# The end of a mixture-of-experts layer: products of the last two pairs in another order, the last norm on other engines, the branch behind the output

## The chip, the cores and the metric

The kernel runs on one core of a Trainium2 chip. The metric is device time in microseconds (us), lower is better. A core has five engines with a queue each: TensorE (PE, with its weight loads as PEld), VectorE (DVE), ScalarE (ACT), GpSimd (POOL) and SyncE (SP), which here issues the DMAs. Matrix products write to PSUM, eight banks of 128 x 512 float32; all else lies in SBUF.

## What is computed

One layer over 256 rows of 1024 numbers: a mixer (gated linear attention and retention), a layer norm, a mixture of 32 experts of which each row takes four, and a last layer norm. The end of it is what the change touches:

```python
h = layer_norm(DEEPNORM_ALPHA * h + mix, ln1_g[l], ln1_b[l])
ffn = moe_ffn(h, router_w[l], router_b[l], moe_w1[l], moe_b1[l], moe_w2[l], moe_b2[l])
h = layer_norm(DEEPNORM_ALPHA * h + ffn.astype(h.dtype), ln2_g[l], ln2_b[l])

# one expert e with the rows xb that chose it
hh = xb @ w1[e] + b1[e]                                  # 1024 -> 2048
x_glu = jnp.minimum(hh[:, :D_FF], SWIGLU_LIMIT)
x_lin = jnp.clip(hh[:, D_FF:], -SWIGLU_LIMIT, SWIGLU_LIMIT)
act = x_glu * jax.nn.sigmoid(SWIGLU_ALPHA * x_glu) * (x_lin + 1.0)
return act @ w2[e] + b2[e]                               # 1024 -> 1024, then times the gate, summed over experts
```

The weights of the experts are 32 x (8 MB + 4 MB) of float32, some 403 MB of the 424 MB that the kernel moves.

## The kernel before

**Pairs.** Two experts make a pair; there are 16, and each expert has 64 seats (CAP), so that a pair fills 128 partitions. For a pair p the work is: `begin` (`gather`, L746) picks the rows by products with a 0/1 matrix; `hidden` is the first product, 8 steps k of 4 blocks of 512 columns, each block a `pair_product` (L767), which is two float32 matmuls that stand side by side in 64 output rows each; `activate` (L813 to L817, DVE and ACT) is the clamped SwiGLU; `turn` (L824, L825) transposes the result on PE and copies it out on ACT; `outputs` is the second product, 4 steps g of 2 x 2 `pair_product`s into two banks, copied to `y` by ACT (L842); `gated` (L850 to L856) makes the transposed gates, and `scatter` (L879, L883) multiplies them with `y` and adds the result to the sum `acc`, 256 rows in two tiles t. The scatter of pair p - 1 (`finish`) runs inside the first product of pair p, after its step k = 1.

**What sets the order.** `in_order` chains all PE work in the order of the program's text. The other engines are ordered by a scheduler that works from dependencies, and `tc.issue_after` forces the order of two instructions where it is used.

**The stream.** SP issues the weights as DMAs of 1 MB (L960 for w1, L962 for w2; one of each expert makes a step), eight in flight, into 20 slots of 1 MB that come round as a ring; a slot is free again when the products that read it are done.

**The last pair before.** Its w2 comes in 24 smaller pieces (L987): first all of the columns 0:512 in 8 pieces of 512 KB, then 512:768 and 768:1024 in 16 pieces of 256 KB (rows of 1 KB), so that a column block of the result is finished before the next one has arrived. Each block is evicted (L1000, L1013), scattered and put through the statistics of the last norm (L886) in turn.

**The branch and the last norm.** An expert with more than 64 rows needs further rounds. All engines load a count (`values_load`, L1017) and branch (`tc.If(count > CAP)`, L1022) over the code for these rounds; with the inputs here none is needed. Behind the branch stands the last norm (L1060 to L1078): aggregate, logarithm and exponential, a Newton step (`newton`, L173 to L177), then four tiles of 128 x 512, three of them on DVE (two instructions each, L1077 and L1078), one on ACT and POOL (L1072 to L1074), and an output DMA for each (L1079). L1119 is the end of the program, where the engines meet.

Of the kernel before, what the change touches and what calls it, by code (L numbers as in the profile page):

```python
# [33 lines left out]
WARM = (10, 8, 6)  # L34
NS = 20
# [8 lines left out]
def tile_layer(ctx: ExitStack, tc: tile.TileContext, x, positions, rows_d, bc_d, gate_d, w_in, wglr_d,  # L44
# [736 lines left out]
    def hidden(xg, sel2, load, name, mid=None, early=None, bias_last=False):  # L781
# [20 lines left out]
        if mid:  # L802
            mid()
        aT = mp.tile([P, KC, P], F32, name="aT" + name, tag="aT")
        for turn in turns_:
            turn(aT)
        return aT, bsel, sigs[-1]

    def activate(hf, ps, name):
# [3 lines left out]
        V.tensor_scalar(glu, pglu, 7.0, None, op0=ALU.min)  # L813
# [3 lines left out]
        V.scalar_tensor_tensor(glu, plin, 1.0, glu, op0=ALU.add, op1=ALU.mult)  # L817
# [3 lines left out]
        def turn(aT):  # L821
            pa = bank("y", f"pa{name}{hf}").rearrange("p (k s) -> p k s", k=4)
# [6 lines left out]
    def outputs(aT, bsel, load, name):  # L829

        y = mp.tile([P, D], F32, name="y" + name, tag="y")
        py = [bank("y", f"py{name}{n}") for n in range(2)]
        for n in range(2):
            set_bias(py[n], bsel, 4 + n)
        for g in range(4):
            ws = [load("w2", i, g) for i in range(2)]
            for k in range(2):
                for n in range(2):
                    pair_product(py[n], aT, 2 * g + k, [w.rearrange("p (k n) -> p k n", k=2)[:, k, n * 512:(n + 1) * 512] for w in ws],
                                 g == 3 and k == 1)  # L840
        for n in range(2):
# [29 lines left out]
    st2 = const.tile([P, NT, 4, 6], F32, name="st2")  # L871
# [3 lines left out]
    def scatter(y, gT, at, n, name, stats=False, tag="m", first=False):  # L875

        for t in range(NT):
# [6 lines left out]
            if stats:  # L884
                for c in range(at, at + n, 256):
                    V.bn_stats(st2[:, t, c // 256, :], acc[:, t, c:c + 256])  # L886
# [67 lines left out]
    for p in range(NP):  # L954
        nm = f"_{p}"

        def load(what, i, g):
            w = slot(next_slot(), f"{what}{nm}{i}_{g}")
# [6 lines left out]

        if p:
# [3 lines left out]
        if p == NP - 2:  # L970
            kept = next_slot()
            gb2 = row_slot(kept, G2, "gb2")
        aT, bsel, last_sig = hidden(xgs[p], sel[:, 2 * p:2 * p + 2], load, nm, mid=(lambda: begin(p + 1)) if p + 1 < NP else None,
                                    early=lambda: middle(p), bias_last=(p == 0))
        if p + 1 < NP:
            ys[p] = outputs(aT, bsel, load, nm)
            continue

        loads = []

        def load_pair(ws, w, k0, m, c_):

            n, w_k = ws[0].shape[-1], ws[0].shape[1]
            for kq in range(0, w_k, m):
                for i in range(2):
                    with tc.issue_after(loads[-1].ins) if loads else ExitStack():
                        loads.append(nc.sync.dma_start(  # L987
                            ws[i][:, kq:kq + m, :],
                            w[0, 2 * p + i][(k0 + kq) * P:(k0 + kq + m) * P, c_:c_ + n].rearrange("(p k) n -> p k n", p=P)))

        preload(EXPLN, last_sig)
        y = mp.tile([P, D], F32, name="y" + nm, tag="y")
        py = bank("y", "py_last0")
        set_bias(py, bsel, 4)
        for kh in range(2):
            ws = [slot(next_slot(), f"w2{nm}{i}_0{kh}").rearrange("p (k n) -> p k n", k=4) for i in range(2)]
            load_pair(ws, moe_w2, 4 * kh, 2, 0)
            for k in range(4):
                pair_product(py, aT, 4 * kh + k, [w[:, k, :] for w in ws], kh == 1 and k == 3)
        A.activation(y[:, 0:512], py, AF.Copy)  # L1000
        for q in range(2):
            at = 512 + 256 * q
            py = bank("y" if q == 0 else "h", f"py_last{q + 1}")[:, 0:256]
            ws = [slot(next_slot(), f"w2{nm}{i}_1{q}").rearrange("p (k n) -> p k n", k=8) for i in range(2)]
            load_pair(ws, moe_w2, 0, 2, at)
            set_bias(py, bsel, 5, 256 * q)
            for k in range(8):
                if q == 0 and k == 4:
                    scatter(y, gTs[p], 0, 512, nm, stats=True)
                if q == 1 and k == 6:  # L1010
                    scatter(y, gTs[p], 512, 256, nm, stats=True)
                pair_product(py, aT, k, [w[:, k, :] for w in ws], k == 7)
            A.activation(y[:, at:at + 256], py, AF.Copy)  # L1013
        scatter(y, gTs[p], 768, 256, nm, stats=True)
# [5 lines left out]
    free = [s_ for s_ in ring if s_ != kept]  # L1020
    chain[0] = None
    with tc.If(count > CAP):  # L1022
        for r in range(1, S // CAP):
            V.tensor_scalar(pos, pos, -float(CAP), None, op0=ALU.add)
            with tc.For_i(0, NP, 1) as p:
# [16 lines left out]
                aT, bsel, _ = hidden(xg, sel[:, 0:2], load, nm)  # L1042
                y = outputs(aT, bsel, load, nm)
# [3 lines left out]
                for tl in (pos, gate, sel):  # L1047
# [4 lines left out]
                    V.tensor_copy(tl, tmp)  # L1052
        for t in range(NT):
            for c in range(4):
                V.bn_stats(st2[:, t, c, :], acc[:, t, c * 256:(c + 1) * 256])
        preload(EXPLN, A.activation(nmr2, st2[:, 0, 0, 0:1], AF.Copy))


    for t in range(NT):
# [63 lines left out]
```

## Time and profile before

| | us |
|---|---|
| time, median of 3 runs (1083.78 to 1084.68) | 1084.24 |
| the profiled execution: its time | 1084.73 |
| the profiled execution: its span in the trace | 1082.9 |
| PE busy (share of the span) | 1009.8 (93%) |
| DVE busy | 273.1 (25%) |
| ACT busy | 168.9 (16%) |
| POOL busy | 36.1 (3%) |
| moved by DMA, 424.17 MB, mean GB/s | 392 |

All times of the trace are us from the start of the span. "Busy" is the time in which an engine executes; the granted clock is what the chip allows TensorE, 1.00 for 2.4 GHz and 0.50 for 1.2 GHz. A row of a timeline gives start, duration, engine, line, operation, what is written and read, the shapes and how many instructions it groups; in brackets stands the idle time before it and what ended that. A matmul of float32 leaves two records, and a `pair_product` four.

### The profile page before, as it was taken

What the parts mean: (1) busy time and instruction counts of PE and PEld (TensorE: products, weight loads), DVE (VectorE), ACT (ScalarE), POOL (GpSimd) and SP (SyncE); (2) the same over time, 40 slices, a digit from 0 to 9 for tenths busy, and PEclk for the clock granted to TensorE, in tenths of its full rate; (3) what the DMA queues carried; (4) which work ended last, traced back from release to release, by engine and by line L of the source; (5) the groups of instructions that cost most, each with busy time, mean ns of one, the idle gap of its engine ahead of it and who ended that gap; (6) DMA issues with size and microseconds to landing.
All of it is one profiled execution on the core that took longest, in us unless ns stands there. A gap on an engine that the chain in (4) does not pass through costs nothing. (4 is left out here: it accounts for less than half of the span.)

```text
span 1082.9 us, 11976 instructions
## 1 busy us (share of the span) xinstructions
PE 1009.8 (93%) x4870; PEld 457.6 (42%) x4870; DVE 273.1 (25%) x574; ACT 168.9 (16%) x350; POOL 36.1 (3%) x90
## 2 busy tenths in 40 slices
PE   8999999999999999999989899998989898999974
PEld 6989844343434342434333243433333332434322
DVE  5667832121212123212120111212121101212114
ACT  3755521010101010101010010101010010101010
POOL 2001100000000000000000000000000000000001
PEclk9999999999999998999999999999999999989997
DMA  9866789999999999999999999999999999999993
GB/s 340 312 238 223 303 339 419 420 420 420 419 419 419 420 419 419 419 419 419 420 420 419 421 420 419 419 419 419 420 420 420 419 419 420 420 419 419 419 371 118
DMA packets 70706, 424.17 MB, mean 392 GB/s; under 512 B 7300, under 2 KB 11887, under 8 KB 22511
## 3 DMA queue, kind: packets, MB, share of 16 engines
q1 hardware_dynamic: 70496, 422.78, 95.9%
q8 instruction: 40, 0.66, 0.3%
q10 hardware_dynamic: 146, 0.53, 0.1%
q14 instruction: 24, 0.20, 0.1%
HBM read 421.71 MB, written 1.05 MB: 390 GB/s over the span
## 5 line engine op out<-in xcount | busy, mean ns | idle before, releaser
L767 PE MATMUL ph<-w,xg 128*64 128x512 f32 x2048 | 469.3, 601 | 31.1 <-DMA w<-in_moe_w_dram 31.1
L767 PEld LDWEIGHTS ph<-w,xg 128*64 128x64 f32 x2048 | 152.0, 138 | 338.9 <-issue 270.2
L767 PE MATMUL py<-w,aT 128*64 128x512 f32 x960 | 218.2, 613 | 0.0
L883 DVE TENSOR_TENSOR acc<-acc,po 128x512 f32<-128x512 f32 (+1 forms) x62 | 41.6, 671 | 391.5 <-PE po L879 391.4
L767 PEld LDWEIGHTS py<-w,aT 128*64 128x64 f32 x960 | 69.7, 141 | 138.9 <-issue 138.4
L813 DVE TENSOR_SCALAR glu<-ph 128x512 f32<-128x512 f32 x32 | 22.0, 687 | 333.5 <-PE ph L767 314.5
L814 ACT ACTIVATE ph<-glu 128x512 f32<-128x512 f32 x32 | 19.3, 602 | 540.2 <-DVE glu L813 540.2
L746 PEld LDWEIGHTS px<-hot,res 128*128 128x128 f32 x512 | 58.4, 192 | 12.5 <-DVE glu L816 10.6
L746 PE MATMUL px<-hot,res 128*128 128x128 f32 x512 | 61.6, 278 | 0.7 <-DVE hot L752 0.7
L879 PE MATMUL po<-y,gT 128*128 128x512 f32 (+1 forms) x132 | 59.8, 594 | 0.5 <-ACT y L1013 0.5
L842 ACT ACTIVATE y<-py 128x512 f32<-128x512 f32 x30 | 17.9, 598 | 217.5 <-PE py L767 217.5
L879 PEld LDWEIGHTS po<-y,gT 128*128 128x128 f32 x132 | 23.6, 189 | 36.0 <-issue 34.9
L759 ACT ACTIVATE xg<-px,cols 128x128 f32<-128x128 f32 x64 | 24.1, 458 | 44.6 <-PE px L746 44.6
L773 PE MATMUL py<-bt,bsel 64*128 64x512 f32 x30 | 14.8, 498 | 16.9 <-ACT aT L825 16.9
L778 POOL CAST bsel<-sel 128x128 fp32r<-128x128 f32 x16 | 4.7, 291 | 634.1 <-PE py L773 624.2
L815 DVE TENSOR_SCALAR ph<-ph 128x512 f32<-128x512 f32 x32 | 22.2, 694 | 2.2 <-PE ph L767 1.2
L761 DVE TENSOR_SCALAR xg<-px,cols 128x128 f32<-128x128 f32 x64 | 21.8, 403 | 3.4 <-PE px L746 3.4
L824 PE MATMUL pa<-ident,glu 128*128 128x128 f32 x128 | 18.6, 286 | 3.8 <-DVE glu L817 3.8
L817 DVE SCALAR_TENSOR_TENSOR glu<-ph,glu 128x512 f32<-128x512 f32 x32 | 22.0, 686 | 0.7
L816 DVE TENSOR_TENSOR glu<-glu,ph 128x512 f32<-128x512 f32 x32 | 21.6, 678 | 0.9 <-ACT ph L814 0.7
L850 POOL TENSOR_TENSOR hog<-hot,gate 128x128 f32<-128x128 f32 x32 | 12.6, 415 | 218.5 <-PE pg L854 205.1
L824 PEld LDWEIGHTS pa<-ident,glu 128*128 128x128 f32 x128 | 16.7, 207 | 5.3 <-DVE glu L817 5.3
(290 smaller groups left out, 658.9 us busy)
## 6 DMA issues: line engine op xcount, KB each, us to landing
w<-in_moe_w_dram SPq DMA_DIRECT2D x376, 1024.0 KB, 19.9
w_out<-in_w_out_dram SPq DMA_DIRECT2D x4, 1024.0 KB, 8.0
w<-in_moe_w_dram SPq DMA_DIRECT2D x8, 512.0 KB, 15.7
w<-in_moe_w_dram SPq DMA_DIRECT2D x16, 256.0 KB, 6.2
w_gqk<-in_w_in_dram SPq DMA_DIRECT2D x2, 1024.0 KB, 9.5
w_rqk<-in_w_in_dram SPq DMA_DIRECT2D x2, 1024.0 KB
w_gv<-in_w_in_dram SPq DMA_DIRECT2D x2, 1024.0 KB, 10.6
w_rv<-in_w_in_dram SPq DMA_DIRECT2D x2, 1024.0 KB, 14.4
```

Of the source, the lines that this page charges most:

```text
L746: in_order(lambda: T.matmul(px[c // 4][:, c % 4, :], res[:, t, c * P:(c + 1) * P], hot[:, t, :], start=(t == 0 and c % 4 == 0), stop=(t == ...
L759: lasts["xa"] = A.activation(xg[:, c, :], px[c // 4][:, c % 4, :], AF.Identity, bias=bs, scale=gs)
L761: lasts["xv"] = V.tensor_scalar(xg[:, c, :], px[c // 4][:, c % 4, :], gs, bs, op0=ALU.mult, op1=ALU.add)
L767: in_order(lambda: T.matmul(ps[i * CAP:(i + 1) * CAP, :], lhs[:, k, i * CAP:(i + 1) * CAP], ws[i], start=first, stop=last, skip_group_chec ...
L813: V.tensor_scalar(glu, pglu, 7.0, None, op0=ALU.min)
L814: sig = A.activation(pglu, glu, AF.Sigmoid, scale=1.702)
L815: V.tensor_scalar(plin, plin, 7.0, -7.0, op0=ALU.min, op1=ALU.max)
L816: V.tensor_mul(glu, glu, pglu)
L817: V.scalar_tensor_tensor(glu, plin, 1.0, glu, op0=ALU.add, op1=ALU.mult)
L824: in_order(lambda: T.transpose(pa[:, k, :], units[:, k // 2, k % 2, :], ident))
L879: in_order(lambda: T.matmul(po[:, 0:n], gT[:, t, :], y[:, at:at + n], start=True, stop=True))
L883: V.tensor_add(acc[:, t, at:at + n], acc[:, t, at:at + n], po[:, 0:n])
```

## The change

The diff below stands for these edits:

- The order of the last two pairs is now: first product of pair 14, first product of pair 15, second product of pair 14, second product of pair 15. What waits meanwhile is held in `waiting`; the transposes of pair 14 go into pair 15's first product after k = 1 (through banks of tag "m"), those of pair 15 into the middle of pair 14's second product (`between`), to a slot of the ring (`ay_last`).
- The w2 of pair 15 comes in four whole DMAs of 1 MB (half the rows), then the other half of the rows in 6 pieces of 512 KB and 4 of 256 KB that have 512 columns each (rows of 2 KB).
- The columns 512:1024 of the sum are gathered in two PSUM banks, `fused`: identity times `acc`, plus the scattered results of pair 14, plus those of pair 15. The statistics read these banks.
- The last norm leaves POOL out. For the tile t = 1 PE multiplies the centred rows by a diagonal matrix `dg` of the reciprocal deviations on top of the bias row (in `pz`), and ACT copies the result out; for t = 0 DVE does both steps. Ten transposes with no use for the result stand ahead of it on PE (`WARM2`).
- The outputs go out before the count is loaded and the branch is taken; ACT first copies `fused` to `acc` for the rounds behind the branch, and a second copy of the norm stands there.
- In all pairs the DVE instructions of the second half of `activate` are forced behind those of the first.

```diff
-        aT = mp.tile([P, KC, P], F32, name="aT" + name, tag="aT")
-        for turn in turns_:
-            turn(aT)
-        return aT, bsel, sigs[-1]
+        return turns_, bsel, sigs[-1]
...
-        V.tensor_scalar(glu, pglu, 7.0, None, op0=ALU.min)
+        with tc.issue_after(last_act[0].ins) if hf else ExitStack():
+            V.tensor_scalar(glu, pglu, 7.0, None, op0=ALU.min)
...
+        def early():
+            if p < NP - 1:
+                middle(p)
+            else:
+                waiting[0:0] = turned(waiting.pop(0), waiting[-1], "m")
...
+        if p < NP - 2:
+            ys[p] = outputs(*turned(turns_, nm), biased(bsel, nm), load, nm)
+        elif p == NP - 2:
+            waiting = [turns_, biased(bsel, nm), load, nm]
...
+    fused = [bank("m", f"fused{t}") for t in range(NT)]
+    def between():
+        both.extend(turned(turns_, nm, "h", slot(next_slot(), "ay_last")))
+        for t in range(NT):
+            in_order(lambda: T.matmul(fused[t], ident, acc[:, t, 512:D], start=True, stop=False, skip_group_check=True))
+    ys[L - 1] = outputs(*waiting, between=between)
...
+    for g in range(2):
+        ws = [load("w2", i, g).rearrange("p (k n) -> p k n", k=2) for i in range(2)]
+        for k in range(2):
+            for n in range(2):
+                pair_product(py[n], aT, 2 * g + k, [w[:, k, cs[n]] for w in ws])
+        if g == 0:
+            scatter(y_old, gTs[L - 1], 0, 512, "_old", tag="y")
+            for t in range(NT):
+                in_order(lambda: T.matmul(fused[t], gTs[L - 1][:, t, :], y_old[:, 512:D], start=False, stop=False, skip_group_check=True))
...
+        for k in range(4):
+            if n and k == 2:
+                scatter(y, gTs[L], 0, 512, "_last", stats=True, tag="y")
+            pair_product(py[n], aT, 4 + k, [w[:, k, :] for w in ws], k == 3)
+        A.activation(y[:, cs[n]], py[n], AF.Copy)
+    for t in range(NT):
+        in_order(lambda: T.matmul(fused[t], gTs[L][:, t, :], y[:, 512:D], start=False, stop=True, skip_group_check=True))
+        V.bn_stats(st2[:, t, 1, :], fused[t])
...
+    for _ in range(WARM2):
+        in_order(lambda: T.transpose(warm2[:, 0:P], ident, ident))
...
+        centre(1, 0)
+        after(lambda: newton(r, small("ln2_w" + name, 2, "_w"), ve))
+        A.activation(dg, ident, AF.Copy, scale=r[:, 1:2])
+        centre(1, 1)
+        for n in range(2):
+            in_order(lambda: T.matmul(pz[n], dg, u[:, 1, cs[n]], start=False, stop=True, skip_group_check=True))
+            lasts["out"] = A.activation(ob[:, 1, cs[n]], pz[n], AF.Copy)
+            nc.sync.dma_start(out[0, P:2 * P, cs[n]], ob[:, 1, cs[n]])
+        for n in range(2):
+            centre(0, n)
+            after(lambda: V.scalar_tensor_tensor(ob[:, 0, cs[n]], u[:, 0, cs[n]], r[:, 0:1], gb2[:, 1, cs[n]], op0=ALU.mult, op1=ALU.add))
+            nc.sync.dma_start(out[0, 0:P, cs[n]], ob[:, 0, cs[n]])
...
+    norm_out(lambda t, n: fused[t] if n else acc[:, t, cs[0]], "")
+    with tc.issue_after(lasts["out"].ins):
+        for t in range(NT):
+            A.activation(acc[:, t, 512:D], fused[t], AF.Copy)
     count = nc.values_load(routed[0][0:1, 0:1], min_val=0, max_val=S)
```

Where PE stands between the pairs 14 and 15 before: `px` is the gather of pair 15, `pa` the transposes and `py` the second product of pair 14 (`w_140` and `w_141` are weights of its two experts, `aT` its activated rows).

```order
L746 MATMUL px_5099<-hot_5096,res 128x128 x4
L824 MATMUL pa_5127<-ident,glu_5084 128x128 x4
L824 MATMUL pa_5133<-ident,glu_5090 128x128 x4
L773 MATMUL py_5140<-bt,bsel_4954 128x512
L773 MATMUL py_5141<-bt,bsel_4954 128x512
L767 MATMUL py_5140<-w_140_0_5144,aT_5126 64x512
L767 MATMUL py_5140<-w_141_0_5146,aT_5126 64x512
```

The same place on PE with the change: `pg` are the gates and `ph` the first product of pair 15 (`w_150`, `w_151`).

```order
L747 MATMUL px_5099<-hot_5096,res 128x128 x4
L774 MATMUL py_5126<-bt,bsel_4954 128x512
L774 MATMUL py_5127<-bt,bsel_4954 128x512
L869 MATMUL pg_5133<-ident,hog_5130 128x128 x2
L774 MATMUL ph_5140<-bt,bsel_5138 128x512
L774 MATMUL ph_5141<-bt,bsel_5138 128x512
L774 MATMUL ph_5142<-bt,bsel_5138 128x512
L774 MATMUL ph_5143<-bt,bsel_5138 128x512
L768 MATMUL ph_5140<-w_150_0_5148,xg_5097 64x512
L768 MATMUL ph_5140<-w_151_0_5150,xg_5097 64x512
```

Behind the gather PE now goes on with the first product of pair 15, and the transposes of pair 14 have left this place.

The end of PE's work before, from the last two matmuls of the last pair's last block on:

```order
L767 MATMUL py_last_5417<-w_150_11_5418,aT_5332 64x256
L767 MATMUL py_last_5417<-w_151_11_5419,aT_5332 64x256
L879 MATMUL po_5454<-y_5346,gT_5200 128x256
L879 MATMUL po_5458<-y_5346,gT_5200 128x256
L1017 TENSOR_LOAD mosti
L1022 COMPARE_AND_BRANCH
```

The same with the change:

```order
L768 MATMUL py_last_5339<-w_150_c_5389,ay_last 64x512
L768 MATMUL py_last_5339<-w_151_c_5390,ay_last 64x512
L1049 MATMUL fused_5271<-ay_last,gT_5136 128x512
L1049 MATMUL fused_5272<-ay_last,gT_5136 128x512
L1057 MATMUL pz_5418<-gb_4952,ones 128x512
L1057 MATMUL pz_5419<-gb_4952,ones 128x512
L1060 MATMUL warm_5422<-ident 128x128 x10
L1087 MATMUL pz_5418<-u,dg 128x512
L1087 MATMUL pz_5419<-u,dg 128x512
L1102 TENSOR_LOAD mosti
L1107 COMPARE_AND_BRANCH
```

The part of the norm that is now PE's, its bias rows and the ten transposes stand between the last scatter and the branch.

The end of SP's queue before; the branch L1022 stands ahead of all these rows, right behind the last weights, and the L1038 and L1025 rows are the code that it jumps over:

```order
L1038 DMA w_r_3_6224<-in_moe_w_dram 128x2048
L1025 REGISTER_ALU
L1025 COMPARE_AND_BRANCH
L1025 UNCONDITIONAL_BRANCH
L1022 UNCONDITIONAL_BRANCH x2
L1079 DMA out_dram<-acc 128x512 x4
L1119 UNCONDITIONAL_BRANCH
```

The end of SP's queue with the change, from the last weights on:

```order
L1042 DMA w_150_c_5389<-in_moe_w_dram 128x512
L1042 DMA w_151_c_5390<-in_moe_w_dram 128x512
L1093 DMA out_dram<-out 128x512
L1089 DMA out_dram<-out 128x512 x2
L1093 DMA out_dram<-out 128x512
L1107 COMPARE_AND_BRANCH
L1110 COMPARE_AND_BRANCH
L1110 UNCONDITIONAL_BRANCH x2
```

The outputs now follow the weights, and the jump is SP's last step instead of one between the two.

## Rows read from the trace of the kernel before

**Rows 1.** Windows: stretch, length, busy us by engine, granted clock, DMA share, GB/s.

```profile
961.40:968.10 6.70, 6.70 (x15) 1.55 (x15) 0.00 (x0) 1.19 (x2) 0.00 (x0) 0.50 1.02 419
980.00:1036.00 56.00, 52.59 (x248) 21.19 (x244) 9.18 (x16) 5.15 (x11) 0.29 (x1) 1.00 1.01 418
1038.00:1046.00 8.00, 6.25 (x28) 2.14 (x24) 3.38 (x6) 0.68 (x2) 0.00 (x0) 1.00 1.03 384
1052.00:1062.00 10.00, 10.00 (x57) 4.13 (x53) 2.44 (x6) 0.60 (x1) 0.00 (x0) 1.00 0.97 308
1062.00:1066.00 4.00, 4.00 (x31) 2.49 (x29) 0.43 (x3) 0.39 (x1) 0.00 (x0) 1.00 0.14 42
1066.00:1070.50 4.50, 2.45 (x14) 1.16 (x12) 2.92 (x8) 0.38 (x1) 0.00 (x0) 1.00 0.02 5
1070.50:1083.00 12.50, 0.00 (x0) 0.00 (x0) 7.14 (x14) 1.22 (x3) 3.04 (x2) 0.50 0.24 87
```

**Rows 2.** Timeline of PE, pairs 14 and 15.

```profile
954.85 3.70 PE L879 MATMUL po<-y,gT 128*128 128x512 f32 x8
958.48 4.56 PE L868 MATMUL gb<-gb,ones 1*128 1x512 f32 x8
...
989.97 1.12 PE L824 MATMUL pa<-ident,glu 128*128 128x128 f32 x8
...
993.19 13.95 PE L767 MATMUL py<-w,aT 128*64 128x512 f32 x64
...
1036.29 3.65 PE L767 MATMUL ph<-w,xg 128*64 128x512 f32 x16 [1.33 <-DMA w<-in_moe_w_dram]
1041.31 3.65 PE L767 MATMUL ph<-w,xg 128*64 128x512 f32 x14 [1.37 <-DMA w<-in_moe_w_dram]
...
1066.23 1.08 PE L767 MATMUL py_last<-w,aT 128*64 128x256 f32 x8
1067.83 1.13 PE L879 MATMUL po<-y,gT 128*128 128x256 f32 x4 [0.51 <-ACT y L1013]
```

**Rows 3.** Timeline of DVE, from the last block's statistics to the last output.

```profile
1069.33 0.74 DVE L886 BATCH_NORM_STATS2 st<-acc 128x6 f32<-128x256 f32 x2
1070.77 0.39 DVE L1060 BATCH_NORM_AGGREGATE mv<-st 128x2 f32<-128x24 f32 x2 [0.69 <-DVEq L1022]
...
1071.93 0.34 DVE L173 SCALAR_TENSOR_TENSOR ln_w<-ln_y,ln_v 128x1 f32<-128x1 f32 x2
1072.99 0.23 DVE L177 SCALAR_TENSOR_TENSOR ln_y<-ln_w,ln_y 128x1 f32<-128x1 f32 x2 [0.72 <-DVE ln_w L173]
...
1073.92 0.74 DVE L1078 SCALAR_TENSOR_TENSOR acc<-acc,ln_y,gb 128x512 f32<-128x512 f32 x1
1074.59 1.75 DVE L1077 SCALAR_TENSOR_TENSOR acc<-acc,mv,gb 128x512 f32<-128x512 f32 x1
1076.26 2.40 DVE L1078 SCALAR_TENSOR_TENSOR acc<-acc,ln_y,gb 128x512 f32<-128x512 f32 x2
```

**Rows 4.** By line L1079: the output DMAs, min/median/max ns, and their landing.

```profile
L1079 SPq DMA_DIRECT2D out_dram<-acc x4: 332/352/387, 1074.7 to 1079.1; - x4
...
DMA to landing us min/median/max: 2.0/2.1/2.1
```

**Rows 5.** Page part 5: the copy of a bank by ACT, busy and mean ns.

```profile
L842 ACT ACTIVATE y<-py 128x512 f32<-128x512 f32 x30 | 17.9, 598 | 217.5 <-PE py L767 217.5
```

**Rows 6.** By line L1022, the branch: min/median/max ns, first and last start.

```profile
L1022 SPq EVENT_SEMAPHORE  x8: 17/17/17, 1064.4 to 1064.9; - x8
...
L1022 SPq COMPARE_BRANCH   x1: 50/50/50, 1058.8 to 1058.8; - x1
...
L1022 PEldq COMPARE_BRANCH  x1: 3737/3737/3737, 1068.4 to 1068.4; - x1
L1022 DVEq COMPARE_BRANCH  x1: 76/76/76, 1070.1 to 1070.1; - x1
L1022 DVEq EVENT_SEMAPHORE  x1: 21/21/21, 1070.7 to 1070.7; - x1
```

More of the change, by code (lines that the diff above doesn't have):

```diff
@@ L779, in selector, with hidden @@
         return bsel
-    def hidden(xg, sel2, load, name, mid=None, early=None, bias_last=False):
+    def hidden(xg, sel2, load, name, early=None, bias_last=False):
         bsel = selector(sel2, name)
@@ L827, in activate, with biased, outputs @@
         return turn, sig
-    def outputs(aT, bsel, load, name):
-        y = mp.tile([P, D], F32, name="y" + name, tag="y")
-        py = [bank("y", f"py{name}{n}") for n in range(2)]
+    def biased(bsel, name, tag="y"):
+        py = [bank(tag, f"py{name}{n}") for n in range(2)]
         for n in range(2):
             set_bias(py[n], bsel, 4 + n)
+        return py
+    def outputs(aT, y, py, load, name, between=None):
         for g in range(4):
@@ L840, in outputs @@
                                  g == 3 and k == 1)
+            if g == 1 and between:
+                between()
         for n in range(2):
@@ L952, in middle, with loader @@
             gains(gb2)
-    for p in range(NP):
-        nm = f"_{p}"
+    def loader(p, name):
         def load(what, i, g):
-            w = slot(next_slot(), f"{what}{nm}{i}_{g}")
+            w = slot(next_slot(), f"{what}{name}{i}_{g}")
             if what == "w1":
@@ L964, in load @@
             return w
+        return load
+    waiting = None
+    for p in range(NP):
+        nm = f"_{p}"
+        load = loader(p, nm)
         if p:
@@ L972, in tile_layer @@
             gb2 = row_slot(kept, G2, "gb2")
-        aT, bsel, last_sig = hidden(xgs[p], sel[:, 2 * p:2 * p + 2], load, nm, mid=(lambda: begin(p + 1)) if p + 1 < NP else None,
-                                    early=lambda: middle(p), bias_last=(p == 0))
-        if p + 1 < NP:
[L976 to L984, printed above, removed]
+        def early():
+            if p < NP - 1:
+                middle(p)
+            else:
+                waiting[0:0] = turned(waiting.pop(0), waiting[-1], "m")
@@ new lines, in tile_layer @@
+        turns_, bsel, last_sig = hidden(xgs[p], sel[:, 2 * p:2 * p + 2], load, nm, early=early, bias_last=(p == 0))
+        if p + 1 < NP:
+            begin(p + 1)
+        if p < NP - 2:
+            ys[p] = outputs(*turned(turns_, nm), biased(bsel, nm), load, nm)
+        elif p == NP - 2:
+            waiting = [turns_, biased(bsel, nm), load, nm]
+    preload(EXPLN, last_sig)
+    L = NP - 1
+    aT, y = None, None
+    both = []
+    fused = [bank("m", f"fused{t}") for t in range(NT)]
[3 more added lines that the diff above has]
+            in_order(lambda: T.matmul(fused[t], ident, acc[:, t, 512:D], start=True, stop=False, skip_group_check=True))
@@ new lines, in tile_layer @@
+    ys[L - 1] = outputs(*waiting, between=between)
+    aT, y = both
+    y_old = ys[L - 1]
+    py = biased(bsel, "_last", "h")
+    cs = [slice(n * 512, (n + 1) * 512) for n in range(2)]
+    for g in range(2):
[7 more added lines that the diff above has]
+                in_order(lambda: T.matmul(fused[t], gTs[L - 1][:, t, :], y_old[:, 512:D], start=False, stop=False, skip_group_check=True))
@@ L991, in tile_layer @@
[L991 to L1013, printed above, removed]
@@ L1019, in tile_layer @@
     w2r = moe_w2[0].rearrange("e d n -> (e d) n")
-    free = [s_ for s_ in ring if s_ != kept]
+    free = [s_ for s_ in ring if s_ not in (kept, done_slot, spare)]
     chain[0] = None
@@ L1040, in load @@
                     return w
-                aT, bsel, _ = hidden(xg, sel[:, 0:2], load, nm)
-                y = outputs(aT, bsel, load, nm)
+                turns_, bsel, _ = hidden(xg, sel[:, 0:2], load, nm)
+                y = outputs(*turned(turns_, nm), biased(bsel, nm), load, nm)
                 for n in range(2):
```

85 lines of the change are left out of this document (50 added, 35 removed).

## The prediction, made before the changed kernel ran

> **What bounds the kernel now.** I read the stages first, in the windows, and then the timelines from the last weights to the end. From 980 to 1036 us the DMA engines are busy all the time at 418 GB/s [rows 1], and PE waits for each step of weights: its work on the last steps of pair 15's first product starts at 1036.29 and 1041.31, each time behind a wait of 1.3 us for a load [rows 2]. So a step of two loads takes 5.0 us, and until the stream ends nothing but the stream counts.
>
> The last pair's second product is another stage. Between 1052 and 1062 PE is busy without a gap while the stream falls to 308 GB/s on its 1 KB rows [rows 1]. The last product ends at 1066.23 + 1.08 = 1067.3 [rows 2]. From there to the last output issue at 1079.1 nothing is streamed: 11.8 us of copies, statistics and norm, with DVE as the engine that is never done [rows 3, 4]. Then 3.8 us more: 2.1 until the output has landed (1081.2) and 1.7 in which the engines meet [rows 4]. The change touches these three stretches: the order at the stream's end, the tail, and what follows the last issue.
>
> **The order of the last two pairs.** The bytes and their rate stay, so the step that lands at 1041.3 is still the 20th of the 24 steps of the last two pairs; it becomes the last step of pair 14's second product instead of pair 15's first, and activation and transposes of pair 15 move ahead of it, under the stream. Is PE back at the stream by then? It starts pair 15's first product when it now starts pair 14's second one (993.19), since the two transposes of 1.12 us and a wait give way to six small products. The step for it landed at about 986.3 (5.0 us a step back from 1041.3), so PE is 7 us behind. A step of four pair products takes 4 x 0.87 = 3.5 us (13.95 us for 16 [rows 2]), so each gains 1.5 us, less 1.1 for the moved transposes; after six of the twelve steps PE waits for loads again. The cover for the moved work is this slack; without it, it would cost its own 1.1 us twice.
>
> The first step of pair 15's w2 lands 5.0 us later, at 1046.3. From there PE is the bound: 16 pair products, 13.95 us, and six full matmuls of 128 x 512 (two each for the old scatter, the old half in `fused`, the last scatter) at 3.70 / 4 = 0.92 us [rows 2], 5.55. I add 0.2 for switches: the last product ends at **1066.0, 1.3 us earlier**. The stream must keep ahead of that. Before, the last pair's 8.4 MB came half in pieces of 512 KB and half in pieces of 256 KB, 10.9 us at 384 GB/s and 13.6 at 308, and it ended at about 1062 (a DMA share of 0.97 up to there and 0.14 behind [rows 1]). Now half of it comes whole, 10.0 us at 418 GB/s, and half in rows of 2 KB, 10.9 us at 384 or, at worst, 13.6 at 308: an end 3.6 or 0.9 us earlier, 1058.4 or 1061.1. PE wants the last pieces two pair products and a little before 1066.0, at about 1064. So PE stays the bound at either rate, and this edit is worth 1.3 us. Were the stream late, by a step of the ring for instance, each us of it would cost one.
>
> **The tail.** Before, from the last product's end to the start of the aggregation: 1070.77 - 1067.31 = 3.5 us, of which 0.69 is the branch [rows 3]. Now the copy takes 0.60 for 512 columns [rows 5] and 0.15 to be seen (the copy of 256 kept PE waiting 0.51, of which 0.38 were work [rows 2]); two matmuls into `fused` 0.92 each; the second statistics 0.74 (the 512 columns of the L886 row [rows 3]): 1066.0 + 0.75 + 1.85 + 0.75 = 1069.35, nearly the same distance. Statistics that read PSUM do not stand in the trace; I take the price from SBUF, and between 0 and 0.2 us more each for the range.
>
> From the aggregation to the last issue it took 1079.1 - 1070.77 = 8.3 us. In it stand a stall of 0.72 within the Newton step, and DVE tiles that took 1.75 and 1.2 us while POOL worked, against 0.74 before (and 0.66 from start to start) [rows 3]. Now: aggregation, logarithm and exponential 1.15 us as before (1070.77 to 1071.93); a Newton step on two columns at once, three instructions of under 0.2 (two take 0.23 to 0.34), to 1071.0; then five DVE tiles at 0.66 (the second centring of t = 1, then two and two for t = 0): 1074.3. PE and ACT work beside it: `dg` to 1071.5 (no more than the 0.60 of a copy four times as wide [rows 5]), two products of 0.92, copies of 0.75: 1074.1. Both arms end together, and I put the last issue at **1074.5, 4.6 us earlier** than 1079.1. POOL's share is then DVE's and PE's, which costs less than it gave.
>
> **The branch behind the output.** This is the price. Before, SP took its branch at 1058.8 and went on at 1064.4, 5.6 us later, while it had nothing to do anyway [rows 6]; PE's took 3.74 us, hidden too; DVE went on after 0.6 us (1070.1 to 1070.7) and its second stall in the Newton step may belong to the same jump. Each price fell under other work, save DVE's. Now SP can branch only when the last output is issued: 1074.5 + 0.35 [rows 4] = 1074.9. Nothing covers it but the landing of the outputs, 2.1 us. What SP's jump costs with an idle queue, no row shows: 0.6 is the floor (DVE) and 5.6 the ceiling (SP, under the full stream). I take PE's **3.74**, since its jump at 1068.4 was made with the DMA engines nearly idle (5 GB/s [rows 1]), as SP's will be, and since both jump over the code of the further rounds.
>
> The sum: 1074.9 + 3.75 = 1078.65; the semaphores behind the branch 0.5 (1064.4 to 1064.9 [rows 6]); the meeting 1.7: 1080.85 against a span of 1082.9. So the ends give back 2.5 of the 4.6 us and **2.05 us** are left. The profiled execution took 1084.73; it would be 1082.7. The median of the runs is 0.49 lower, 1084.24, and from it I forecast **1082.2 us**.
>
> The Trainium skill ("Runtime: NRT & Kernel Launch", Instruction fetch mechanics) says that a taken branch whose target is not in the current two-page window forces a DMA fetch of the page before execution can go on. It speaks against this change: it makes a jump behind the outputs a fetch on the path, as my 3.74 has it, and by it the first rival below would not happen. DVE's 0.6 us [rows 6] shows that not every jump here waits that long, so the rows leave that rival open.
>
> ACT's copies of `fused` for the rounds behind the branch (two of 0.6) and ACT's and PE's own branches come before SP's jump ends: PE's last product at 1073.3 + 0.5 for the count + 3.74 = 1077.6. They cost nothing, and would cost up to 1 us if SP's jump were short. The forced order of DVE in all pairs delays a second half by 0.2 us at most where PE waits for loads; nothing.
>
> **The rivals.**
>
> *The jump is short* (0.18). If SP's page is at hand, as DVE's was, the landing sets the end: 1074.5 + 2.1 + 1.7 = 1078.3, a gain of 4.6, 1079.6; with PE's own jump as the last instead (1077.6 + 0.5 + 1.7) 1079.8, a gain of 3.1, 1081.1. For it speaks DVE's row; against it that SP and PE both waited.
>
> *The gain is given back at the end* (0.20). SP's jump takes 5.6 as it did: 1074.9 + 5.6 + 0.5 + 1.7 = 1082.7, a gain of 0.2, 1084.0. Or the clock falls just ahead of `pz`: its two products take 1.85 each, the last copy ends at 1071.5 + 3.7 + 0.75 = 1075.95, 1.45 later than forecast, 1083.65. For the first speaks SP's own row, against it the stream that it shared the DMA engines with.
>
> *The clock falls early* (0.07; slower). In pair 14 four products with a single row of weights ran 4.56 us without a gap, and behind them the granted clock was 0.50 from 961.4 to 968.1 [rows 1, 2]; at the end of before it is 0.50 from 1070.5 on. The changed kernel puts two such one-row products on PE right behind `fused`, and PE has paused for the copy just before. If the clock falls as `fused` ends (1068.6), the bias rows take 2 x 1.85, the ten transposes 10 x 0.28 (twice the 1.12 / 8 of the `pa` row), `pz` 2 x 1.85: 1078.8, the copy 1079.55, 5.05 us later than forecast, a span of 1085.9: **1087.2**. It decides from a last issue after 1078.7, that is if the clock is down before the transposes begin. Against it: before, the clock held until 1070.5, 1.5 us behind PE's last work, and here PE pauses for under 1 us at a time.
>
> The Trainium skill ("TensorE: Matmul & The Clock Gate", Part 1) has the clock follow how busy PE has been, and by that a PE that works without a gap would keep it and this rival fall away; the drop behind 4.56 us of unbroken one-row products [rows 1, 2] differs from that, and the measurement decides.
>
> **How the numbers follow.** What a measurement of this kernel can tell from no change is about 0.2%, 2.17 us: 1082.07 and 1086.41 are the bounds. The forecast (0.52) spans 1081.2 to 1083.4: 1.0 us better if SP's jump costs 2.7, 1.2 worse if it costs 4.5 and the statistics out of PSUM 0.2 more each. The bound lies just beside its middle; I give 0.24 of it to faster and 0.28 to no change. The short jump adds 0.18 to faster, the gain given back 0.20 to no change, the early clock 0.07 to slower; of 0.03 for the rest 0.01 goes to no change and 0.02 to slower. So faster 0.42, no change 0.49, slower 0.09. The range 1080.3 to 1084.4 leaves out the early clock, half of the short jump, and the rest: not quite 2 in 10.
>
> **What would show it.** The order: PE's first work on w2 of pair 15 at about 1046.3, no wait for loads after it, the last product's end at 1066.0. The tail: aggregation at 1069.4, DVE tiles of 0.66 to 0.74 throughout, the last output issue at 1074.5. The branch: SP's branch row at 1074.9 and its semaphore row behind it, 3.7 us later; that distance, between 0.6 and 5.6, settles most. The clock: 1.00 until `pz` is done. The prediction is wrong if PE waits for pieces beyond 1060, if the distance at SP lies outside its bounds, or if the clock falls before 1071.

## The result, and the profile after

The changed kernel takes **1069.84 us** (median of 4 runs, 1068.21 to 1070.19), the one before 1084.46 on the same chip: a ratio of 0.9864, interval 0.985 to 0.9878, 14.6 us less. The forecast was 2.05 us less, 1082.2, with a range of 1080.3 to 1084.4. The sign of its sum came out and the size did not: the time lies 10 us below the range. The experiments show that the whole gain comes from something that the prediction never priced, and that the edits which it did price are worth nothing together. That the time fell at all is luck.

First the profile. Where the kernel before moved 418 to 420 GB/s through the middle of its span ([rows 1] has 418 for 980 to 1036), the changed kernel moves 427. The windows (stretch, length, busy us by engine, granted clock, DMA share, GB/s), first one of the kernel before:

```profile
500.00:600.00 100.00, 94.36 (x434) 37.49 (x432) 19.15 (x36) 10.31 (x22) 2.10 (x6) 0.98 1.01 419
```

Then the changed kernel, two from the middle and three from the end:

```profile
500.00:600.00 100.00, 97.62 (x468) 38.70 (x466) 19.36 (x36) 10.30 (x22) 2.09 (x6) 1.00 1.01 427
600.00:700.00 100.00, 93.05 (x442) 38.32 (x440) 16.63 (x32) 10.29 (x22) 2.09 (x6) 1.00 1.01 427
...
1050.00:1054.60 4.60, 3.88 (x13) 1.16 (x12) 2.68 (x5) 0.60 (x1) 0.00 (x0) 1.00 0.00 0
1054.60:1059.60 5.00, 4.96 (x19) 2.40 (x18) 4.83 (x12) 1.41 (x4) 0.00 (x0) 1.00 0.01 3
1059.60:1068.40 8.80, 0.00 (x0) 0.00 (x0) 0.95 (x2) 1.57 (x3) 0.00 (x0) 0.62 0.35 127
```

At 500 us nothing of the change has run yet but the order of two halves on DVE, and the DMA engines are busy all the time in both kernels; yet the bytes come 1.8% faster. Over the some 850 us in which the stream sets the pace that is 15 us. The packets, the pieces in which a DMA engine moves the data, say the same: the mean of the 8 KB packets between 400 and 900 us is 314.9 ns before (a fifth take 320 or more) and 309.4 ns after, where 99.9% take 309 or 310.

The end of the changed kernel, PE first, then DVE:

```profile
1031.48 4.35 PE L768 MATMUL py_last<-w,ay_last 128*64 128x512 f32 x16
...
1050.04 1.94 PE L768 MATMUL py_last<-w_c,ay_last 128*64 128x512 f32 x8
1052.70 1.98 PE L1049 MATMUL fused<-ay_last,gT 128*128 128x512 f32 x4 [0.72 <-ACT ay_last L1047]
...
1057.67 1.89 PE L1087 MATMUL pz<-u,dg 128*128 128x512 f32 x4
```

```profile
1055.45 0.21 DVE L1066 BATCH_NORM_AGGREGATE mv<-st 128x2 f32<-128x12 f32 x1
...
1057.61 0.74 DVE L1079 SCALAR_TENSOR_TENSOR u<-acc,mv,gb 128x512 f32<-128x512 f32 x1
1058.39 0.75 DVE L1092 SCALAR_TENSOR_TENSOR out<-u,ln_y,gb 128x512 f32<-128x512 f32 x1
...
1059.84 0.75 DVE L1092 SCALAR_TENSOR_TENSOR out<-u,ln_y,gb 128x512 f32<-128x512 f32 x1
```

and the output DMAs and the branch by line (min/median/max ns, first and last start), which answer to [rows 4, 6]:

```profile
L1089 SPq DMA_DIRECT2D out_dram<-out x2: 384/704/1024, 1059.6 to 1060.7; - x2
...
L1093 SPq DMA_DIRECT2D out_dram<-out x2: 348/367/386, 1059.2 to 1061.2; - x2
...
DMA to landing us min/median/max: 2.6/3.8/4.9
...
L1107 SPq EVENT_SEMAPHORE  x8: 17/17/17, 1064.9 to 1067.1; - x8
...
L1107 DVEq COMPARE_BRANCH  x1: 76/76/76, 1060.7 to 1060.7; - x1
...
L1107 SPq COMPARE_BRANCH  x1: 50/50/50, 1061.7 to 1061.7; - x1
...
L1107 DVEq EVENT_SEMAPHORE  x1: 21/21/21, 1063.8 to 1063.8; - x1
```

From the last product's end (1050.04 + 1.94 = 1051.98) to the end of the span (1068.5) are 16.5 us, where the kernel before needed 1082.9 - 1067.3 = 15.6. By the prediction's sum this part was to shrink to 14.85 (1080.85 - 1066.0); it has got longer.

### The profile page after: what moved, and what is told of

Read it like the earlier page. It is cut to its first block, busy times and chain, and to the rows that moved or that the text cites. A ratio compares the mean times of both kernels' runs of the same rounds, so it can differ in the third digit from the quotient of the medians.

```text
span 1068.5 us, 11926 instructions
## 1 busy us (share of the span) xinstructions
PE 1010.1 (95%) x4855; PEld 459.0 (43%) x4855; DVE 269.1 (25%) x562; ACT 170.3 (16%) x353; POOL 33.2 (3%) x88
## 4 chain that ended last, share of the span: by engine, by line
PE 65%; DMA 30%; ACT 2%; DVE 2%; issue 1%; POOL 0%; ACTq 0%; SPq 0%
DMA w<-in_moe_w_dram 30%; PE ph L768 28%; PE py L768 13%; PE px L747 3%; PE po L894 3%; PE pm L587 2%; PE p_gate L283 2%; PE py_last L768 1%; PE p_gqk L283 1%; PE p_gv L383 1%; PE p_rqk L283 1%; PE p_rv L383 1%; ACT xg L760 1%; PE py L774 1%; PE gb L165 1%; PE ph L774 1%
## 5 line engine op out<-in xcount | busy, mean ns | idle before, releaser
L768 PE MATMUL ph<-w,xg 128*64 128x512 f32 x2048 | 464.4, 600 | 20.5 <-DMA w<-in_moe_w_dram 20.5
L898 DVE TENSOR_TENSOR acc<-acc,po 128x512 f32<-128x512 f32 x52 | 35.8, 688 | 344.0 <-PE po L894 344.0
L894 PE MATMUL po<-y,gT 128*128 128x512 f32 x112 | 51.8, 605 | 0.0
L894 PEld LDWEIGHTS po<-y,gT 128*128 128x128 f32 x112 | 20.1, 189 | 31.5 <-issue 31.5
L774 PE MATMUL py<-bt,bsel 64*128 64x512 f32 x30 | 14.6, 508 | 15.6 <-ACT aT L835 15.4
```

What stands on the lines that cost most here:

```text
L768: in_order(lambda: T.matmul(ps[i * CAP:(i + 1) * CAP, :], lhs[:, k, i * CAP:(i + 1) * CAP], ws[i], start=first, stop=last, skip_group_chec ...
L774: in_order(lambda: T.matmul(ps, bsel[r0:r0 + 64, :], bt[r0:r0 + 64, nb // 2, at:at + ps.shape[-1]], start=not last, stop=last, skip_group_ ...
L894: in_order(lambda: T.matmul(po[:, 0:n], gT[:, t, :], y[:, at:at + n], start=True, stop=True))
L898: V.tensor_add(acc[:, t, at:at + n], acc[:, t, at:at + n], po[:, 0:n])
```

## Experiments on the rate of the stream

What else is different at 500 us? The weight ring's 20 slots lie behind the constant tiles in SBUF, and the change alters these: `st2` has half its columns (96 bytes a partition less), and the small tiles of the norm and its second copy add 64. So in the built program the slots begin at byte 38144 of a partition instead of 38176. The change to `st2` is not among the lines of the diff shown with the change:

```diff
-    st2 = const.tile([P, NT, 4, 6], F32, name="st2")
+    st2 = const.tile([P, NT, 2, 6], F32, name="st2")
```

The theory was that this place sets the rate, the rival that an edit of the change does. Four kernels moved the slots by making `st2` longer and changed nothing else (the few small tiles that lie between `st2` and the slots move with them):

```diff
-    st2 = const.tile([P, NT, 4, 6], F32, name="st2")
+    st2 = const.tile([P, 56], F32, name="st2")[:, 0:48].rearrange("p (t c s) -> p t c s", t=NT, c=4)
```

This is `b_pad32`; `b_pad64` takes 64 columns, and `a_pad32` and `a_pad64` do the same to the changed kernel's `st2`.

> The kernel before, with the tile st2 32 bytes a partition longer, so that the 20 slots of the weight ring begin 32 bytes further on: at byte 38208 of a partition (a multiple of 64) instead of 38176 (32 more than a multiple of 64). Nothing else moves. Theory 1, the slots' place sets the rate of the stream: packets of 8 KB in 309 ns as in the changed kernel instead of 315, 427 GB/s instead of 419, and about 1070.5 us. Theory 2, an edit of the change (the forced order on DVE, the order of the pairs) made the stream faster: 1084.4 us, 419 GB/s.

> The changed kernel with st2 32 bytes longer: its slots begin at byte 38176 as those of the kernel before did, instead of 38144. Theory 1 (place): the stream falls back to 419 GB/s and packets of 315 ns, about 1083.5 us; what is left between this and the kernel before is what the change's own edits are worth. Theory 2 (an edit): 1069.8 us, 427 GB/s.

> The kernel before with st2 64 bytes longer: the slots move as well, to byte 38240, but are again 32 bytes past a multiple of 64. Theory 1 in this form: 1084.4 us, no change. If any move helps, or if what counts is the distance to something else than a multiple of 64, the time falls towards 1070 us.

> The changed kernel with st2 64 bytes longer: slots at byte 38208, a multiple of 64 but not of 128 (38144 was a multiple of 256). If 64 bytes are what counts: 1069.8 us, no change. If 128 or 256 bytes count: about 1083.5 us.

`a_pad32` came as theory 1 (the place) had it: the changed kernel with slots at the old place takes 1084.66 us (ratio to the kernel before 1.0003, 0.9993 to 1.0013). The whole gain is gone. `b_pad32` gave 1083.53 and `a_pad64` 1083.24, both with the slots at a multiple of 64: there theory 1 failed in its first form, since this is not enough. `b_pad64`, which was to stay at 1084.4, gave 1082.98. So these moves alone do little; the next two asked for 256 and 128. In `b_less32` the kernel before gets the changed kernel's place:

```diff
-    mv2 = const.tile([P, NT, 2], F32, name="mv2")
-    nmr2 = const.tile([P, 1], F32, name="nmr2")
+    mvn = const.tile([P, 5], F32, name="mv2")
+    mv2, nmr2 = mvn[:, 0:4].rearrange("p (t c) -> p t c", t=NT), mvn[:, 4:5]
```

> The kernel before with two small tiles of its last norm (mv2, nmr2) put into one, so that the slots begin 32 bytes earlier, at byte 38144 as in the changed kernel (a multiple of 256); b_pad32 had moved them to another multiple of 64 without effect. Theory 1, now with 128 or 256 bytes instead of 64: packets of 309 ns, 427 GB/s, about 1070 us. Theory 2 (the changed program, not the place): 1083 to 1084.5 us.

> The kernel before with st2 96 bytes longer: slots at byte 38272, a multiple of 128 but not of 256. If a multiple of 128 is what counts: about 1070 us; if 256: 1083 to 1084.5 us, and only b_less32 is fast; if the place is not what counts: 1083 to 1084.5 us for both.

`b_less32` takes **1069.25 us** (ratio 0.9857, 0.9833 to 0.988): the kernel before, with two tiles of 20 bytes in all put into one, is as fast as the changed kernel. `b_pad96`, at a multiple of 128, takes 1081.89: slow, though 1.1 us under what was expected of it and 3 us under the kernel before in the same runs, of which its packets (314.0 ns instead of 314.9) account for some 2.5 over 850 us, an estimate. A last kernel tells a rule from a lucky address; it is `b_less32` with one constant tile put behind the slots:

```diff
+    behind = pool(ctx, "behind")
...
-    seats = const.tile([P, CAP], F32, name="seats")
+    seats = behind.tile([P, CAP], F32, name="seats")
```

> The kernel of b_less32 with one constant tile of 256 bytes (seats) put behind the slots instead of ahead of them: slots at byte 37888, 256 bytes below 38144 and a multiple of 512. If a multiple of 256 is what counts: as b_less32, packets of 309 ns and 1069.3 us. If only the place 38144, or an odd multiple of 256, is fast: 1082 to 1084.5 us.

`b_seats` takes 1070.92 us, and so the other multiple of 256 is fast too. The window 500 to 600 us of, in this order, `a_pad32`, `b_pad96`, `b_less32` and `b_seats`:

```profile
500.00:600.00 100.00, 93.62 (x438) 37.95 (x436) 19.36 (x36) 10.30 (x22) 2.09 (x6) 1.00 1.01 420
```

```profile
500.00:600.00 100.00, 95.94 (x438) 37.65 (x436) 19.15 (x36) 10.31 (x22) 2.10 (x6) 0.97 1.01 421
```

```profile
500.00:600.00 100.00, 97.63 (x460) 38.55 (x457) 18.76 (x36) 10.29 (x22) 2.10 (x6) 0.98 1.01 427
```

```profile
500.00:600.00 100.00, 97.61 (x460) 38.53 (x458) 19.16 (x36) 10.31 (x22) 2.10 (x6) 0.98 1.01 427
```

The DMA share is 1.01 in all four: it cannot show the loss, because a packet that takes longer counts as busy. The GB/s show it. By place, with the mean 8 KB packet:

| slots begin at byte | multiple of | kernel | packet, ns | median us |
|---|---|---|---|---|
| 38176 | 32 | before | 314.9 | 1084.46 to 1085.02 |
| 38176 | 32 | changed (`a_pad32`) | 314.9 | 1084.66 |
| 38208 | 64 | before (`b_pad32`) | 314.1 | 1083.53 |
| 38208 | 64 | changed (`a_pad64`) | 314.0 | 1083.24 |
| 38240 | 32 | before (`b_pad64`) | 314.0 | 1082.98 |
| 38272 | 128 | before (`b_pad96`) | 314.0 | 1081.89 |
| 38144 | 256 | before (`b_less32`) | 309.4 | 1069.25 |
| 38144 | 256 | changed | 309.4 | 1069.84 |
| 37888 | 512 | before (`b_seats`) | 309.4 | 1070.92 |

The packet follows the place and not the kernel: all places tried that are a multiple of 256 are fast (two), the four others are not. And where both kernels stand at one place, they differ by -0.3 to +0.6 us: the edits that the prediction priced at -2.05 are worth nothing together. Why packets to the other places take longer (how a row of 8 KB is cut on its way into SBUF, say) no run shows.

## Experiments on the end

`a_pad32` has the old place and the old rate, so it is the kernel that the prediction described. Its rows, PE and the lines of the output and the branch:

```profile
1045.22 4.64 PE L768 MATMUL py_last<-w,ay_last 128*64 128x512 f32 x16
...
1064.08 1.94 PE L768 MATMUL py_last<-w_c,ay_last 128*64 128x512 f32 x8
```

```profile
L1089 SPq DMA_DIRECT2D out_dram<-out x2: 382/858/1333, 1073.6 to 1075.1; - x2
...
L1093 SPq DMA_DIRECT2D out_dram<-out x2: 348/362/375, 1073.2 to 1075.6; - x2
...
DMA to landing us min/median/max: 2.9/3.7/4.6
...
L1107 SPq EVENT_SEMAPHORE  x8: 17/17/17, 1079.3 to 1081.6; - x8
...
L1107 SPq COMPARE_BRANCH   x1: 50/50/50, 1076.0 to 1076.0; - x1
```

| step | predicted | `a_pad32` |
|---|---|---|
| last product ends | 1066.0 | 1066.0 |
| last output issued | 1074.5 | 1075.6 |
| SP branches | 1074.9 | 1076.0 |
| SP's first semaphore behind the branch | 1078.65 | 1079.3 |
| end of the span | 1080.85 | 1083.0 |

Work ends as forecast; what is lost stands around the branch. From the last product's end to the end of the span it is 17.0 us instead of 15.6: the 1.3 us that the new order gains are lost again there. One output issue takes 1.33 us instead of 0.35, the semaphores behind the jump take 2.3 us instead of 0.5, and the outputs land up to 4.6 us after their issue instead of 2.1. Leaving the branch out of both kernels shows its price in each place. `a_nobranch` and `b_nobranch` are the changed kernel and `b_less32` without the count, the branch and the rounds (in `a_nobranch` also without ACT's two copies ahead of them and the second norm), all with slots at byte 38144:

```diff
-    count = nc.values_load(routed[0][0:1, 0:1], min_val=0, max_val=S)
...
-    with tc.If(count > CAP):
...
```

> The changed kernel without the branch and the rounds behind it (left out: the rounds for experts with more than 64 rows, which these inputs do not need) and without ACT's two copies ahead of it; slots at byte 38144. Theory: the jump on SP and what follows it cost the 7.3 us between the last output issue and the end, against 3.8 before; without it 3.8 us, so 1066.2 us. If the slow output issue of 1.3 us on SP is the branch's code too, one us less, 1065.2. Rival: the landing and the meeting of the engines take that long anyway (the landing 3 us instead of 2): 1069 to 1070 us.

> The kernel of b_less32 (the kernel before, slots at byte 38144) without the branch and the rounds behind it (left out: the rounds for experts with more than 64 rows). Theory: ahead of the norm the branch costs only DVE's two stalls, 0.7 us each, so 1.4 us less than b_less32, 1067.8 us; against a_nobranch (1064.5) the other edits of the change are then worth 3.3 us, about the 3.2 of the prediction's sum without the branch (4.6 less 1.4). Rival: the branch costs as much here as in the changed kernel (5.4 us): 1064 us, and the other edits are worth nothing.

`a_nobranch` takes 1064.46 us, 0.7 under the lower of the times expected: the branch costs **5.4 us** behind the outputs. `b_nobranch` takes 1067.52: it costs 1.7 us ahead of the norm. The rest of the change is then worth 1064.46 - 1067.52 = -3.06 us, and the moved branch takes 3.7 back where the prediction had 1.1 (its 2.5 less the 1.4 of DVE's stalls).

These are differences of medians, and the runs of one kernel spread by 1.5 to 3 us. The traces give them more sharply, since the distance from the last product's end to the end of the span hardly varies: 15.6 to 15.7 us in the kernel before at all its places. The last products of `a_nobranch` (span 1063.1) and `b_nobranch` (span 1064.9):

```profile
1048.92 1.94 PE L768 MATMUL py_last<-w_c,ay_last 128*64 128x512 f32 x8
```

```profile
1049.60 1.08 PE L767 MATMUL py_last<-w,aT 128*64 128x256 f32 x8
```

So this distance is 12.2 and 14.2 us. By it the branch costs **4.3 us** behind the outputs (16.5 - 12.2; 4.7 with the 17.0 of `a_pad32`) and 1.4 ahead of the norm (15.6 - 14.2), so that moving it takes 2.9 (3.3), and the rest of the new tail is worth -2.0, where the prediction had -1.9 (4.6 less 1.3 for the order and 1.4 for the stalls). That the medians' -3.06 lies near its -3.2 with the order is in part luck, because at byte 38144 the order gains nothing: the last product ends at 1050.7 and 1050.8 without the change (`b_nobranch`, `b_less32`) and at 1050.5 to 1052.0 in the six kernels with it.

In `a_nobranch` the issues and landings are short again (the lines of its outputs):

```profile
L1089 SPq DMA_DIRECT2D out_dram<-out x2: 332/354/377, 1058.5 to 1059.1; - x2
DMA to landing us min/median/max: 2.3/2.3/2.3
...
L1093 SPq DMA_DIRECT2D out_dram<-out x2: 348/379/410, 1058.0 to 1059.5; - x2
DMA to landing us min/median/max: 2.1/2.3/2.5
```

So the slow issue, the late landing and the long jump all go with the branch and its code. Can the branch be kept and its price not? Two edits take one long jump each away. `a_actq` issues the outputs on ACT's queue, so that SP branches right behind the weights; `a_loop` writes the rounds as a loop over one copy of the code instead of three copies, so that the jumps are shorter:

```diff
-            nc.sync.dma_start(out[0, P:2 * P, cs[n]], ob[:, 1, cs[n]])
+            lasts["dma"] = (nc.sync if name else nc.scalar).dma_start(out[0, P:2 * P, cs[n]], ob[:, 1, cs[n]])
...
-            nc.sync.dma_start(out[0, 0:P, cs[n]], ob[:, 0, cs[n]])
...
+                    lasts["dma"] = nc.scalar.dma_start(out[0, 0:P, cs[n]], ob[:, 0, cs[n]])
```

```diff
-        for r in range(1, S // CAP):
+        with tc.For_i(0, S // CAP - 1, 1):
             V.tensor_scalar(pos, pos, -float(CAP), None, op0=ALU.add)
...
-                nm = f"_r{r}"
+                nm = "_r1"
```

> The changed kernel with its four output DMAs issued by ACT instead of SP, and ACT's copies for the rounds behind them; SP then branches right behind the last weights, under the stream. Theory (SP's jump behind the outputs sets the end): DVE's jump, 3.6 us from 1074.8 on in the run with slots at 38176, is then the last; 2 to 3 us less than the changed kernel, 1066.8 to 1067.8 us. Rival (the landing sets it): no change, 1069.8 us.

> The changed kernel with its rounds behind the branch as a loop over one copy of their code instead of three copies in a row: the jump over them is a third as long on every engine. Theory (the waits behind the branch are for code that has to be fetched): SP's jump takes 0.6 us instead of 3.3 and DVE's 0.6 instead of 3.6, the landing of the outputs is then the last, 2.5 to 3.5 us less than the changed kernel: 1066.3 to 1067.3 us. Rival (a jump costs what it costs, however far): 1069.8 us.

> The changed kernel with both edits: the rounds as a loop over one copy of their code, and the outputs issued by ACT, so that SP's jump lies under the stream and DVE's is short. Theory A (the branch's price is the fetching of code, and the outputs land late because those fetches run beside them): with no long jump left but PE's, the outputs land 2.1 to 2.5 us after their issue as in a_nobranch; 1065.5 to 1066.3 us. Theory B (the outputs land late for another reason, in a_actq 4.2 us after the last issue): the landing stays the last, 1067.5 to 1068.5 us.

`a_actq` takes 1068.86 us, `a_loop` **1068.03** (1067.85 to 1068.63; ratio to the kernel before 0.983 to 0.9863) and both edits together 1069.04. None is as fast as it was expected to be by the theory that it tested. The branch's rows of `a_loop`:

```profile
L1107 SPq EVENT_SEMAPHORE  x8: 17/17/17, 1063.8 to 1065.1; - x8
...
L1107 DVEq COMPARE_BRANCH  x1: 76/76/76, 1059.5 to 1059.5; - x1
...
L1107 SPq COMPARE_BRANCH  x1: 45/45/45, 1060.6 to 1060.6; - x1
...
L1107 DVEq EVENT_SEMAPHORE  x1: 21/21/21, 1060.1 to 1060.1; - x1
```

The shorter code brought DVE's jump from 3.1 us to 0.6, and the semaphores behind SP's jump from 2.2 us to 1.3; SP's jump itself still took 3.2. The length of the code alone does not decide, for in the kernel before DVE jumped over all three copies in 0.6 us too [rows 6]. In `a_actq` and `a_loop_actq` SP's jump is out of the way, and the last output lands 4.2 us after its issue all the same; here is `a_loop_actq`:

```profile
L1097 ACTq DMA_DIRECT2D out_dram<-out x2: 387/402/416, 1060.6 to 1061.1; - x2
DMA to landing us min/median/max: 3.4/3.8/4.2
```

So theory A of that run falls and theory B holds as to the place, with a time half a us above its range. Behind the jump stands the landing, and taking one away uncovers the other: in `a_loop`, `a_actq` and `a_loop_actq` the last output lands at 1064.6, 1064.8 and 1065.3, 0.4 to 0.5 us before SP's last semaphore of the branch, while in the changed kernel it lands at 1066.1 and that semaphore comes 1.0 later. What makes the landing late is open. In every kernel with a branch behind the outputs the trace has packets of code (the kind that it calls instruction), of 8 and 16 KB, among those of the outputs (one of 16 KB took 1.25 us in `a_loop_actq`, at 1062.6), and the last output packets trail behind the others (some twenty of 512 there, by up to 1.8 us); `a_nobranch` has no such packets until the outputs have landed, and no late landing. That they share an engine and wait for each other is argued, not shown. `a_loop` has the lowest median of the kernels that compute everything, 1.8 us below the changed kernel, though the ranges of their runs overlap (1068.21 is the changed kernel's lowest).

The last run takes the clock. The ten transposes ahead of the norm's products are left out:

```diff
-WARM2 = 10
+WARM2 = 0
```

> The changed kernel without the ten transposes ahead of the norm's products (WARM2 = 0). If they keep nothing up: the granted clock is 1.00 in the two products as before, 1069.8 us. Rival (they hold the clock): the products run at 0.50, 1.9 us longer, of which 1.4 us reach the last output issue: 1071.2 us.

1069.46 us. The rival was right in its mechanism and not in its time (1071.2): the windows show the granted clock at 0.61, a mix of its two levels, in the stretch of the two products, and these take 2.98 us, where they take 1.89 to 1.90 in all seven changed kernels with the transposes.

```profile
1054.50:1056.50 2.00, 1.02 (x3) 0.30 (x2) 1.93 (x6) 0.73 (x3) 0.00 (x0) 1.00 0.00 0
1056.50:1058.50 2.00, 2.00 (x4) 0.52 (x2) 1.93 (x4) 0.60 (x1) 0.00 (x0) 0.61 0.04 8
```

```profile
1053.14 1.98 PE L1057 MATMUL pz<-gb,ones 1*128 1x512 f32 x4
1056.10 2.98 PE L1087 MATMUL pz<-u,dg 128*128 128x512 f32 x4 [0.98 <-ACT dg L1084]
```

From the last product's end to the end of the span it is 17.2 us instead of 16.5, 0.7 more in the trace, which is less than the runs of one kernel differ (1068.2 to 1070.2); the medians do not show it.

## Why the prediction was wrong, point by point

**The stream.** "The bytes and their rate stay" is the step that failed, and with it the time and the range. The bytes stayed. The rate did not, because the change moved the slots by 32 bytes, to a multiple of 256. The cause stands in the line that halves `st2`; the prediction does not speak of that line, and did not ask what lies behind the tile. No rival had anything like it, so no chance was kept for a gain of over 4.6 us, and none of the three signs of being wrong looked at the rate. In the trace of before there was a hint: the packets took 314.9 ns on average, and 7% of them 309 or 310.

**The order of the last pairs.** Right at the old place: last product at 1066.0 against 1066.0, PE never waiting for loads after the first step. PE began the last w2 on the first expert's load at 1045.2 and waited in the middle of the first pair product until 1046.2 for the second's (hence 4.64 us for four products that take 3.65 elsewhere), where 1046.3 was forecast; from there it took 19.8 us for what was summed as 19.7. A hit to the tenth is luck all the same: with the slots at byte 38208 the last product ends 2.2 us earlier with the change (1066.5 in `b_pad32`, 1064.3 in `a_pad64`), and at 38144 no earlier. Why it gains nothing there was not tested.

**The tail.** Right up to the work: the second aggregation at 1069.5 (1069.35 predicted), DVE's last tile done at 1074.6 (1074.3), the last copy on ACT at 1074.2 (1074.1). Statistics read from PSUM took 0.70 us, as from SBUF. DVE's stall within the Newton step, which "may belong to the same jump", did: `b_nobranch` has neither of the two, no idle time ahead of these rows.

```profile
1053.34 0.38 DVE L1019 BATCH_NORM_AGGREGATE mv<-st 128x2 f32<-128x24 f32 x2
...
1054.75 0.28 DVE L177 SCALAR_TENSOR_TENSOR ln_y<-ln_w,ln_y 128x1 f32<-128x1 f32 x2
```

**The branch behind the output.** This is the second step that failed: moving the branch, priced at 1.1 us (2.5 less the 1.4 of the stalls), took 2.9 to 3.3 by the traces. The jump, which "settles most", was the best part: 3.3 us against 3.74, with 0.6 and 5.6 as bounds. What was mis-sized is all around it. Issues were priced at 0.35 and one took 1.33; the semaphores behind the jump were priced at 0.5, from a row whose waits lay under the stream, and took 2.3; landings were priced at 2.1 and took up to 4.6. The terms sum to +0.1 (work) + 1.0 (issue) - 0.4 (jump) + 1.45 (semaphores and meeting together): 2.15 us, the distance from 1080.85 to 1083.0. At an equal place this is the rival "the gain is given back at the end", by another mechanism than the two that it named.

**What the jump waits for.** The rule of the Trainium skill on a taken branch ("Runtime: NRT & Kernel Launch", Instruction fetch mechanics), as the prediction gives it, fits `a_loop`: with one copy of the rounds instead of three DVE's jump fell from 3.1 us to 0.6. SP's 3.2 us over the shorter code, and DVE's 0.6 over the whole code in the kernel before, fit it only if the first target lay outside the window and the second inside, which no run shows.

**The clock.** Forecast at 1.00 until `pz` is done, and so it was. The early fall was given 0.07. `a_nowarm` shows that without the transposes the clock falls while `pz` runs, and that this costs PE 1.1 us. By the Trainium skill ("TensorE: Matmul & The Clock Gate", Part 1), as the prediction read it, a PE that works keeps its clock; in the changed kernel the two one-row products (1.98 us, the same as full ones) with the transposes behind them kept it, and in `a_nowarm` the same products with a pause of 1 us behind them did not, a case that the rule leaves room for. That is one profiled execution against seven.

## What to carry to other kernels

Before an edit's work is priced, ask what it moves in memory: a tile that changes its size shifts all that is allocated behind it, and where a stream sets the pace 32 bytes were worth 1.4% here. An edit at the end is priced more sharply by the distance from the last product to the end of the span than by medians. Read the stream's GB/s and packet times in a stretch that the edit does not touch; if they differ, find the place first and compare kernels at an equal place. A branch behind the last output was not hidden here (4.3 to 4.7 us): it costs by the jump, by the issues beside it and by the landing behind it. Price it with the branch left out, not from a row where it was hidden.

## What was not expected of the hardware

- Loads of 8 KB rows into SBUF took 309.4 ns a packet where the slots began at a multiple of 256 bytes (37888, 38144), with hardly any spread, and 314.0 to 314.9 at four places that were not (38176, 38208, 38240, 38272): 427 against 419 to 421 GB/s. The DMA share was 1.01 in both.
- With a branch behind them, outputs of 256 KB landed 2.4 to 4.9 us after their issue, the slowest of each kernel after 4.0 to 4.9; in `a_nobranch` after 2.1 to 2.5.
- A jump over one copy of the rounds instead of three cost DVE 0.6 us instead of 3.1 (in the kernel before it took 0.6 over three); SP's stayed at 3.2.
